# Two transformer blocks on one core: seven block products in the second feed forward, q and k projected together, and a later `out` in the latent attention

## The chip, the cores and the metric

The kernel runs on one core of a Trainium2 chip, as one program. The time is device microseconds of one execution; a kernel's time is the median of its runs. The engines are TensorE (PE), VectorE (DVE), ScalarE (ACT), GpSimd (POOL) and the queue of SyncE (SP), which issues most transfers. PSUM is the memory that matmuls write, SBUF the memory that all engines work from.

## The reference

The input is x, 512 tokens by 1024 features, in fp32. Two blocks follow each other.

```python
def first_block(x, ...):
    xn = rms_norm(h, norm_mix_pre)
    proj = xn @ w_in
    ...
    o_a = mixer_dilated(qkv_a, pos) @ w_o_a
    o_b = mixer_mla(q_c, kv_c, k_pe, pos, ...) @ w_o_b
    mix = (g_a * o_a + g_b * o_b) @ w_out
    h = h + rms_norm(mix, norm_mix_post)
    hn = rms_norm(h, norm_mlp_pre)
    ff = jnp.square(jax.nn.relu(hn @ w_ff1)) @ w_ff2
    h = h + rms_norm(ff, norm_mlp_post)

def second_block(x, ...):
    ...
    h = h + rms_norm_2(mix, ln_mix_post[l])
    a = rms_norm_2(h, ln_ffn_pre[l])
    ff = (jax.nn.silu(a @ w_ffn_gate[l]) * (a @ w_ffn_up[l])) @ w_ffn_down[l]
    h = h + rms_norm_2(ff, ln_ffn_post[l])
```

Block 1 mixes by a dilated attention (12 heads of 64 in three groups; q and k are rotated in their first 16 features) and by a latent attention (8 heads, 512 keys), and has a feed forward with a hidden width of 4096. Block 2 mixes by four recurrent or attention mixers and has a gated feed forward with a hidden width of 2816, which is 22 tiles of 128.

## The kernel before

The program has four phases: block 1's mixers (`mix1`, `mixers1`), its feed forward (`ffn1`), block 2's mixers (`mix2`) and its feed forward (`ffn2`).

**A matmul in three passes.** Each fp32 operand is kept as a high part and a low part. `mm3` (L318) forms a product as three matmuls into one PSUM tile: high by high (L320), high by low (L321) and low by high (L322). `wload` (L282) brings a weight unit of up to 128x1024 on SP's queue into `wraw` (3 buffers); ACT casts it to `whi` (L300) and DVE subtracts to get `wlo` (L301), five buffers each (`WB`). PSUM has four accumulators `acc` and two tiles each of `mps` and `ops`.

**Feed forward of block 2.** `groups` (L1193) walks over groups of hidden tiles, FF2 = (8, 6, 4, 4). For each tile a gate unit and an up unit of 24 matmuls of 512 columns run; `sink` in `ffn2` (L2194) multiplies by the token scale (DVE L2207), takes silu (ACT L2208), multiplies by the up product (DVE L2214) and splits into `hidh`, `hidl` (ACT L2215, DVE L2216). The units of the next group's first tile (two units) are run ahead, and then the group's down products come: for each column half f and each of four token blocks j one accumulator, whose content `Post.part` moves to `y` in SBUF: ACT copies in group 0 (L595), DVE adds in later groups (L597). The last group's products go through `sink`, `done` and the output transfers of `Post`.

**Block 1's projections.** `proj_qk` (L842) makes q or k of a head group in four chunks, one per 128 tokens: 24 matmuls of 256 columns, ACT's scaling of the result (L852), a rotation of four instructions on POOL (L688 to L691), and, as `turn`, transposes on PE (L860) whose results ACT and DVE copy out. `Fill` (L450) hands the chunks out one at a time between the items of the dilated attention; a chunk's `turn` comes after the next chunk. The numbers in `fills` say how many chunks stand before which item, and PE's order there is the order of the code.

**Latent attention.** Its 32 items (`ItemB`) are a head and a block of 128 queries each. `scores` is one matmul (L1092), then the maximum on DVE (L1095), the exponential on ACT (L1099) and the division on DVE (L1101). `turn`, two steps later, transposes P (PE L1106) into an `mps` tile and copies it to PT (L1107), by DVE for even items and by ACT for odd ones. `out`, one step later, multiplies by v (PE L1122); it does two items at once, on the odd one's step.

```python
            lag = 1 if n < 16 else 2
            while turned < len(items) and turned <= n - lag:
                items[turned].turn()
                turned += 1
            while outed < turned and outed <= n - lag - 1:
                items[outed].out()
                outed += 1
```

## Time and profile before

| | |
|---|---|
| median of 3 runs | 1525.47 us (1524.91 to 1526.32) |
| the profiled execution | 1524.67 us, its span 1522.9 us |
| PE busy | 1478.0 us (97%) |
| DVE busy | 788.6 us (52%) |
| ACT busy | 583.7 us (38%) |
| POOL busy | 246.2 us (16%) |

The span is what the profiler recorded of the execution, from the first instruction to the last. Busy times of engines overlap each other. A PE that is busy all the time still loses time with every matmul it need not do; the duration of one matmul in the trace overlaps its neighbours, so that what one costs is read from the distance of starts.

### The profile page before, as it was taken

The page shows a single profiled execution, that of the slowest core. Times are in us where ns is not written, and L with a number is a line of the kernel's source. Part 1 is how long each engine was busy: PE and PEld are TensorE (multiplying, and loading weights), DVE is VectorE, ACT ScalarE, POOL GpSimd, SP SyncE. Part 2 cuts the span into 40 slices and gives each one's busy share as a digit, 9 for nine tenths or more (in the row PEclk, how much of TensorE's full clock was granted, in tenths as well). Part 3 has the DMA queues.
Part 4 walks back from the last instruction along what each step waited for, and adds up shares of the span by engine and source line. Part 5 has one row for each costly group of instructions (what it writes and reads, how often), then busy time and mean ns, then how long its engine had stood idle before and what let it go on. Part 6 is the DMA issues. An engine that isn't in the chain of part 4 may idle for free.

```text
span 1522.9 us, 21857 instructions
## 1 busy us (share of the span) xinstructions
PE 1478.0 (97%) x8516; PEld 1240.6 (81%) x8520; DVE 788.6 (52%) x1569; ACT 583.7 (38%) x1099; POOL 246.2 (16%) x514
## 2 busy tenths in 40 slices
PE   8999999999999999999998999889999999999997
PEld 7999976678888888888887999667788888888885
DVE  6433367743746533434446686857656441434446
ACT  7344454533325442423225343533535323222222
POOL 0321210000201377203700052411000000000000
PEclk9999999999999999999999999979999999999999
DMA  8332121022225332322324423001124322423232
GB/s 302 132 100 75 45 64 42 33 80 97 90 91 179 119 97 70 119 85 87 110 93 141 146 88 116 32 29 42 42 90 161 124 97 59 136 83 111 83 97 84
DMA packets 54728, 147.37 MB, mean 97 GB/s; under 512 B 9824, under 2 KB 16368, under 8 KB 54624
## 3 DMA queue, kind: packets, MB, share of 16 engines
q1 hardware_dynamic: 52384, 143.38, 28.8%
q10 hardware_dynamic: 1776, 1.85, 0.4%
q8 instruction: 67, 1.10, 0.3%
q0 software_dynamic: 464, 0.74, 0.2%
q14 instruction: 37, 0.30, 0.1%
HBM read 135.12 MB, written 11.06 MB: 96 GB/s over the span
## 4 chain that ended last, share of the span: by engine, by line
PE 87%; DVE 9%; ACT 3%; issue 1%; DMA 1%; SPq 0%; DVEq 0%; ACTq 0%
PE acc L320 25%; PE acc L321 24%; PE acc L322 24%; DVE wlo L301 1%; PE acc L1092 1%; PE ops L1032 1%; PE ops L1122 1%; DVE y L625 1%; PE ops L320 1%; PE ops L322 1%; PE ops L321 1%; ACT whi L300 1%; PE acc L1977 1%; PE ops L1993 1%; PE acc L978 1%
## 5 line engine op out<-in xcount | busy, mean ns | idle before, releaser
L300 ACT CAST whi<-wraw 128x1024 fp32r<-128x1024 f32 (+4 forms) x237 | 234.5, 993 | 486.3 <-PE acc L321 226.6
L301 DVE TENSOR_TENSOR wlo<-wraw,whi 128x1024 fp32r<-128x1024 f32 (+4 forms) x237 | 282.2, 1195 | 233.7 <-ACT whi L300 224.1
L320 PE MATMUL acc<-xh,whi 128*128 128x512 f32 (+1 forms) x920 | 348.4, 380 | 7.2 <-ACT whi L300 5.3
L322 PE MATMUL acc<-xh,wlo 128*128 128x512 f32 (+1 forms) x920 | 343.5, 374 | 1.5 <-DVE wlo L301 1.5
L321 PE MATMUL acc<-xl,whi 128*128 128x512 f32 (+1 forms) x920 | 344.6, 375 | 0.3 <-DVE xl L664 0.3
L320 PEld LDWEIGHTS acc<-xh,whi 128*128 128x128 f32 x920 | 174.4, 190 | 44.1 <-ACT whi L300 7.5
L322 PEld LDWEIGHTS acc<-xh,wlo 128*128 128x128 f32 x920 | 174.2, 189 | 33.3 <-DVE wlo L301 2.1
L321 PEld LDWEIGHTS acc<-xl,whi 128*128 128x128 f32 x920 | 174.6, 190 | 31.7 <-issue 1.0
L320 PE MATMUL acc<-whi,hidh 128*128 128x512 f32 x432 | 169.0, 394 | 0.0
L321 PE MATMUL acc<-wlo,hidh 128*128 128x512 f32 x432 | 168.7, 393 | 0.0
L322 PE MATMUL acc<-whi,hidl 128*128 128x512 f32 x432 | 168.4, 392 | 0.0
L320 PE MATMUL acc<-whi,xh 128*128 128x256 f32 (+2 forms) x448 | 131.3, 293 | 0.2 <-ACT mv L1779 0.2
L321 PE MATMUL acc<-wlo,xh 128*128 128x256 f32 (+2 forms) x448 | 127.9, 285 | 0.0
L322 PE MATMUL acc<-whi,xl 128*128 128x256 f32 (+2 forms) x448 | 127.7, 285 | 0.0
L321 PEld LDWEIGHTS acc<-wlo,hidh 128*128 128x128 f32 x432 | 81.2, 188 | 18.3
L322 PEld LDWEIGHTS acc<-whi,hidl 128*128 128x128 f32 x432 | 81.2, 188 | 18.1
L320 PEld LDWEIGHTS acc<-whi,hidh 128*128 128x128 f32 x432 | 81.2, 188 | 17.9
L320 PEld LDWEIGHTS acc<-whi,xh 128*128 128x128 f32 x448 | 86.1, 192 | 2.8 <-issue 1.1
L321 PEld LDWEIGHTS acc<-wlo,xh 128*128 128x128 f32 x448 | 86.2, 192 | 0.1
L322 PEld LDWEIGHTS acc<-whi,xl 128*128 128x128 f32 x448 | 86.0, 192 | 0.0
L1252 POOL TENSOR_TENSOR relu<-relu 128x512 f32<-128x512 f32 (+1 forms) x37 | 36.9, 1005 | 230.6 <-ACT hidh L1251 226.5
L597 DVE TENSOR_TENSOR y<-acc,y 128x512 f32<-128x512 f32 x48 | 33.1, 689 | 63.1 <-PE acc L322 62.9
(535 smaller groups left out, 2151.9 us busy)
## 6 DMA issues: line engine op xcount, KB each, us to landing
wraw<-in_wp_dram SPq DMA_DIRECT2D x211, 512.0 KB, 3.5
hd<-y SPq DMA_DIRECT2D x24, 256.0 KB, 3.9
hr<-hd SPq DMA_DIRECT2D x12, 512.0 KB, 5.1
hr<-in_xt_dram SPq DMA_DIRECT2D x8, 512.0 KB, 5.5
H<-in_xT_dram SPq DMA_DIRECT2D x8, 256.0 KB, 4.6
wraw<-in_wp_dram SPq DMA_DIRECT2D x16, 128.0 KB, 3.7
gain<-in_gv_dram SPq DMA_DIRECT2D x8, 256.0 KB, 4.1
out_dram<-y SPq DMA_DIRECT2D x8, 256.0 KB, 2.1
```

Of the source, the lines that this page charges most:

```text
L300: ACT.copy(hi[:, s], raw[:, s])
L301: eng.tensor_tensor(lo[:, s], raw[:, s], hi.bitcast(F32)[:, s], op=OP.subtract)
L320: PE.matmul(ps, lhsT=w[0], rhs=x[0], start=first, stop=False)
L321: PE.matmul(ps, lhsT=w[0], rhs=x[1], start=False, stop=False)
L322: PE.matmul(ps, lhsT=w[1], rhs=x[0], start=False, stop=last)
L597: DVE.tensor_tensor(y, ps, y, op=OP.add)
L625: DVE.scalar_tensor_tensor(y, y, self.r[:, i:i + 1], self.hs[i][:, 512 * f:512 * f + 512], op0=OP.mult, op1=OP.add)
L978: PE.matmul(Sv[:, jj, a], lhsT=QKV[g]["q"][a][rr, 128 * j:128 * j + 128], rhs=QKV[g]["k"][a][rr, k0:k0 + W], start=False, stop=(jj == step ...
L1032: PE.matmul(po[:, j % 2, h], lhsT=PTv[0:w, jj, a, b], rhs=QKV[g]["v"][v][0:w, 64 * h:64 * h + 64], start=(b == 0), stop=(b == self.nb - 1))
L1092: PE.matmul(S, lhsT=qT[2 * p + e][0:96, 128 * i:128 * i + 128], rhs=kT[2 * (p % 2) + e][0:96], start=True, stop=True)
L1122: PE.matmul(po[64 * f:64 * f + 64, 128 * i:128 * i + 128], lhsT=VB[kt][:, 64 * h:64 * h + 64], rhs=PT[:, 128 * kt:128 * kt + 128], start=F ...
L1252: POOL.tensor_tensor(a, a, a, op=OP.mult)
```

## The change

Three things are changed.

**Seven products.** FF2 becomes (4, 4, 4, 4, 2, 4). In the first four groups the down product of 512 tokens by 512 hidden features (four tiles) by 1024 columns is cut in halves in each direction, and the eight block products are replaced by seven products of sums of blocks. `Pairs` forms the sums of the activations on POOL, per pair of hidden tiles, and splits them (ACT casts, DVE low parts). `seven` loads four weight quarters into tiles `wq` and forms the sums of them on POOL, in place. Each product has two token blocks of two hidden tiles in three passes. `Post.seven` keeps the seven products in SBUF (copied in group 0, added to in groups 1 to 3), and `Post.joined`, once after group 3, forms the eight outputs from them by 14 sums on POOL.

**q and k.** `proj_qk(g)` projects q and k of a head group at once: four chunks of 24 matmuls of 512 columns rather than eight of 256. Four weight units take the place of two and two. A chunk is turned by four transposes into one `mps` tile, copied out in four pieces. `fills` is adapted so that the same has been projected before each item.

**Order of the latent attention.** `out` of an item comes one step later, and the call of `weights_a` that depends on the count of items done comes with it.

```diff
-FF2 = (8, 6, 4, 4)
+FF2 = (4, 4, 4, 4, 2, 4)
+SEVEN = {"down": range(4)}
...
+        cols = lambda nm: list(range(qkv[nm] + 256 * g, qkv[nm] + 256 * g + 256))
+        for h in range(4):
+            u[f"Aqk{g}", h] = ("w_in", rows(2 * h, 2), cols("q") + cols("k"))
+        c = cols("v")
+        if g == 0:
+            c += list(range(3072, 3104))
+        for h, (k0, n) in enumerate(TMK[len(c)]):
+            u[f"Av{g}", h] = ("w_in", rows(k0, n), c)
...
+        def seven(self, g, i, j, ps):
+            if g == 0 and j == 0:
+                if i in (2, 6):
+                    t = gpool.tile([128, D], F32, name="hr", tag="hr", bufs=2)
+                    ts = [t[:, 0:512], t[:, 512:1024]]
+                elif i == 7:
+                    ts = [u("p7", tag="g") for _ in range(2)]
+                else:
+                    r, f = {1: (0, 0), 3: (0, 1), 4: (2, 0), 5: (2, 1)}[i]
+                    ts = [self.ys[r + t][f] for t in range(2)]
+                self.p[i] = ts
+            s = self.p[i][j]
+            if g == 0:
+                ACT.copy(s, ps)
+            else:
+                DVE.tensor_tensor(s, ps, s, op=OP.add)
+        def joined(self):
+            for j in range(2):
+                more = lambda a, b: POOL.tensor_tensor(self.p[a][j], self.p[a][j], self.p[b][j], op=OP.add)
+                more(6, 1)
+                more(1, 2)
+                more(3, 5)
+                more(7, 6)
+                more(3, 6)
+                more(4, 7)
+                more(5, 7)
...
-        def proj_qk(g, nm):
-            us = wrows(f"A{nm}{g}", 256)
-            res = QKV[g][nm] = [u(f"{nm}T", tag="g"), u(f"{nm}T", tag="g")]
-            tps = {}
+        def proj_qk(g):
+            us = ktiles([wload([(f"Aqk{g}", h)])[0] for h in range(4)], 0, 512)
+            for nm in ("q", "k"):
+                QKV[g][nm] = [u(f"{nm}T", tag="g"), u(f"{nm}T", tag="g")]
+            res = QKV[g]["q"] + QKV[g]["k"]
             for j in range(4):
                 ps = acc()
-                lin_tm(ps[:, 0:256], xs, tokpick(j), us, 0, 256)
-                if j % 2 == 0:
-                    tt = u("tm")
-                t = tt[:, 256 * (j % 2):256 * (j % 2) + 256]
-                ACT.activation(t, ps[:, 0:256], AF.Copy, scale=r_tm[:, j:j + 1])
-                rope(t.rearrange("p (h d) -> p h d", h=4)[:, :, 0:16], rp("ropeA", j, 32), 16, POOL)
+                lin_tm(ps, xs, tokpick(j), us, 0, 512)
+                t = u("tm")
+                ACT.activation(t, ps, AF.Copy, scale=r_tm[:, j:j + 1])
+                rope(t.rearrange("p (h d) -> p h d", h=8)[:, :, 0:16], rp("ropeA", j, 32), 16, POOL)
 
                 def turn(j=j, t=t):
-                    if j % 2 == 0:
-                        tps[j] = mps().rearrange("p (a x) -> p a x", a=2)
-                    tpv = tps[j - j % 2]
-                    for a in range(2):
-                        PE.transpose(tpv[:, a, 128 * (j % 2):128 * (j % 2) + 128], t[:, 128 * a:128 * a + 128], ident)
-                    if j % 2:
-                        for a in range(2):
-                            dst, src = res[a][:, 128 * (j - 1):128 * (j + 1)], tpv[:, a]
-                            if g:
-                                dst = res[a].rearrange("p (r x) -> p r x", r=4)[:, :, 32 * (j - 1):32 * (j + 1)]
-                                src = src.rearrange("p (x r) -> p r x", r=4)
-                            (ACT.copy if a == 0 else DVE.tensor_copy)(dst, src)
+                    tp = mps().rearrange("p (a x) -> p a x", a=4)
+                    for a in range(4):
+                        PE.transpose(tp[:, a], t[:, 128 * a:128 * a + 128], ident)
+                    for a in range(4):
+                        dst, src = res[a][:, 128 * j:128 * j + 128], tp[:, a]
+                        if g:
+                            dst = res[a].rearrange("p (r x) -> p r x", r=4)[:, :, 32 * j:32 * j + 32]
+                            src = src.rearrange("p (x r) -> p r x", r=4)
+                        (DVE.tensor_copy if a % 2 else ACT.copy)(dst, src)
                 yield turn
...
-            fill.plan.extend([proj_v(g), proj_qk(g, "q"), proj_qk(g, "k")])
+            fill.plan.extend([proj_v(g), proj_qk(g)])
         fill.plan.extend([mixed([proj_qr(), proj_vb()], (0, 0, 1, 0, 1, 0, 1, 1)), proj_pair(0)] + [gate(m, "g") for m in order[0:2]])
-        fill(14)
+        fill(10)
         rows_b()
         shared_k()
         items = [ItemA(0, j, e) for j in range(4) for e in range(2)]
         items += [ItemA(g, j, e) for g in (1, 2) for j in (0, 2) for e in range(2)]
         items += [ItemB(p, i, e) for p in range(4) for i in range(4) for e in range(2)]
-        fills = [2, 1, 2, 1, 2, 1, 2, 1] + [3] * 4 + [4, 4, 3, 2]
+        fills = [1] * 8 + [2] * 4 + [4, 4, 3, 2]
         fills += [0] * 32
         turned = outed = 0
-        for n in range(len(items) + 4):
+        for n in range(len(items) + 5):
...
-            while outed < turned and outed <= n - lag - 1:
+            while outed < turned and outed <= n - lag - (1 if n < 16 else 2):
...
+        def pair(self, p, a, b):
+            t0, t1 = HALF
+            x, y = u("sx"), u("sy")
+            POOL.tensor_tensor(x[:, t0], a[:, t1], b[:, t1], op=OP.add)
+            POOL.tensor_tensor(x[:, t1], x[:, t0], a[:, t0], op=OP.subtract)
+            POOL.tensor_tensor(y[:, t0], a[:, t0], a[:, t1], op=OP.subtract)
+            POOL.tensor_tensor(y[:, t1], b[:, t0], x[:, t1], op=OP.subtract)
+            if p[1] == 0:
+                self.first[p[0]] = u("a0h", F32R, tag="g"), u("a0l", F32R, tag="g")
+            a0 = tuple(t[:, HALF[p[1]]] for t in self.first[p[0]])
+            ACT.copy(a0[0], a[:, t0])
+            DVE.tensor_tensor(a0[1], a[:, t0], a0[0].bitcast(F32), op=OP.subtract)
+            bs, xs, ys = (split(t, tag="g", nm="pr") for t in (b, x, y))
+            half = lambda s, t: tuple(v[:, t] for v in s)
+            self.ops[p] = {1: a0, 2: half(bs, t0), 4: half(bs, t1), 5: half(xs, t0), 6: half(xs, t1),
+                           7: half(ys, t0), 3: half(ys, t1)}
+            self.mark = self.mark or last(mybir.EngineType.Activation)
...
+    def seven(nm, g, pairs, post):
+        W = {}
+        for r, f in ((0, 0), (1, 0), (1, 1), (0, 1)):
+            W[r, f] = CTX.up.tile([128, 1024], F32, name="wq", tag="wq", bufs=4)
+            o = UOFF[(nm, g), r, f]
+            with tc.issue_after(pairs.mark):
+                nc.sync.dma_start(out=W[r, f], in_=A["wp"][o:o + 128 * 1024].rearrange("(p n) -> p n", p=128))
+        A0, B0, B1, t = W[0, 0], W[1, 0], W[1, 1], W[0, 1]
+        def parts(raw):
+            hi, lo = (wpool.tile([128, 1024], F32R, name=n, tag=n, bufs=WB[1]) for n in ("whi", "wlo"))
+            ACT.copy(hi, raw)
+            DVE.tensor_tensor(lo, raw, hi.bitcast(F32), op=OP.subtract)
+            return [(hi[:, 512 * i:512 * i + 512], lo[:, 512 * i:512 * i + 512]) for i in range(2)]
+        def weights():
+            yield 1, parts(A0)
+            yield 2, parts(B0)
+            POOL.tensor_tensor(t, B1, t, op=OP.subtract)
+            yield 7, parts(t)
+            POOL.tensor_tensor(t, t, A0, op=OP.add)
+            yield 6, parts(t)
+            POOL.tensor_tensor(B0, B0, t, op=OP.subtract)
+            POOL.tensor_tensor(t, B1, t, op=OP.subtract)
+            yield 4, parts(B0)
+            yield 5, parts(t)
+            yield 3, parts(B1)
+        for i, w in weights():
+            for j in range(2):
+                ps = ops() if i == 7 else acc()
+                for k in range(2):
+                    xh, xl = pairs.ops[g, k][i]
+                    c = slice(128 * j, 128 * j + 128)
+                    mm3(ps, (xh[:, c], xl[:, c]), w[k], k == 0, k == 1)
+                post.seven(g, i, j, ps)
...
+                seven(nm, g, pairs, post)
+                if g + 1 not in SEVEN[nm]:
+                    post.joined()
+                n0 += n
+                continue
...
+            a = sil[m][:, ts]
+            DVE.tensor_tensor(a, a, ps, op=OP.mult)
+            if pairs.add(m, sil[m], ts):
+                return
...
-    with phase("m1", u=10, z=12):
+    with phase("m1", u=11, z=12):
...
-    with phase("f2", u=6):
+    with phase("f2", u=8):
```

How the instructions stand is shown at three places. On PE, in the latent attention (scores L1092, turn L1106, out L1122; L1127, L1141 and L1157 after the change), before the change:

```order
L1106 MATMUL mps_2893<-cstt_72,P_2805 128x128 x4
L1092 MATMUL acc_2900<-kT_526,qT_2562 128x512
L1106 MATMUL mps_2909<-cstt_72,P_2846 128x128 x4
L1117 LDWEIGHTS identb_73
L1117 MATMUL ops_2916<-zero_539,identb_73 128x512
L1122 MATMUL ops_2916<-PT_2851,vb_518 64x128
L1122 MATMUL ops_2916<-PT_2894,vb_518 64x128
```

`out` reads PT_2894, which comes from the turn into mps_2893, with one scores matmul and one turn between the two. After the change, where the turn into mps_2533 is that of PT_2534 (the rows left out are the rest of the earlier `out`):

```order
L1141 MATMUL mps_2533<-cstt_72,P_2449 128x128 x4
L1157 MATMUL ops_2343<-PT_2438,vb_518 64x128
...
L1127 MATMUL acc_2552<-kT_526,qT_2214 128x512
L1141 MATMUL mps_2561<-cstt_72,P_2498 128x128 x4
L1127 MATMUL acc_2568<-kT_527,qT_2217 128x512
L1141 MATMUL mps_2577<-cstt_72,P_2514 128x128 x4
L1152 LDWEIGHTS identb_73
L1152 MATMUL ops_2584<-zero_539,identb_73 128x512
L1157 MATMUL ops_2584<-PT_2503,vb_518 64x128
L1157 MATMUL ops_2584<-PT_2534,vb_518 64x128
```

There two turns and two scores stand between a turn and the `out` that reads it.

On DVE, during a group's down products in block 2's feed forward (L597 evicts an accumulator, L301 makes a low part of weights), before the change:

```order
L597 TENSOR_TENSOR y_10850<-acc_12875,y_10850 128x512
L597 TENSOR_TENSOR y_10852<-acc_12889,y_10852 128x512
L597 TENSOR_TENSOR y_10854<-acc_12903,y_10854 128x512
L301 TENSOR_TENSOR wlo_13036<-wraw_13034,whi_13035 128x1024
L597 TENSOR_TENSOR y_10856<-acc_12917,y_10856 128x512
L301 TENSOR_TENSOR wlo_13072<-wraw_13070,whi_13071 128x1024
L597 TENSOR_TENSOR y_10851<-acc_12943,y_10851 128x512
L597 TENSOR_TENSOR y_10853<-acc_12957,y_10853 128x512
L597 TENSOR_TENSOR y_10855<-acc_12971,y_10855 128x512
L301 TENSOR_TENSOR wlo_13106<-wraw_13104,whi_13105 128x1024
L597 TENSOR_TENSOR y_10857<-acc_12985,y_10857 128x512
```

and after it, in the fourth group, where L624 evicts a product and L1285 and L309 make the low parts of a weight sum and of a loaded weight:

```order
L624 TENSOR_TENSOR y_10504<-acc_12503,y_10504 128x512
L1285 TENSOR_TENSOR wlo_12596<-wq_12489,whi_12595 128x1024
L624 TENSOR_TENSOR hr_11140<-acc_12515,hr_11140 128x512
L624 TENSOR_TENSOR hr_11140<-acc_12523,hr_11140 128x512
L624 TENSOR_TENSOR p7_11162<-ops_12536,p7_11162 128x512
L1285 TENSOR_TENSOR wlo_12616<-wq_12487,whi_12615 128x1024
L624 TENSOR_TENSOR p7_11163<-ops_12544,p7_11163 128x512
L309 TENSOR_TENSOR wlo_12652<-wraw_12650,whi_12651 128x1024
L624 TENSOR_TENSOR hr_11185<-acc_12557,hr_11185 128x512
L624 TENSOR_TENSOR hr_11185<-acc_12565,hr_11185 128x512
L309 TENSOR_TENSOR wlo_12686<-wraw_12684,whi_12685 128x1024
```

Where eight evictions stood among low parts there are fourteen, about two to each low part.

On POOL, which had nothing in this phase, the first group's rows after the change (L1291, L1293, L1295 and L1296 are the sums of weights, L1255 to L1258 those of activations):

```order
L1291 TENSOR_TENSOR wq_11107<-wq_11105,wq_11107 128x1024
L1255 TENSOR_TENSOR sx_10891<-sil_10677,sil_10681 128x256
L1257 TENSOR_TENSOR sy_10892<-sil_10677 128x256
L1256 TENSOR_TENSOR sx_10891<-sx_10891,sil_10677 128x256
L1258 TENSOR_TENSOR sy_10892<-sil_10681,sx_10891 128x256
L1255 TENSOR_TENSOR sx_11013<-sil_10738,sil_10978 128x256
L1257 TENSOR_TENSOR sy_11014<-sil_10738 128x256
L1256 TENSOR_TENSOR sx_11013<-sx_11013,sil_10738 128x256
L1293 TENSOR_TENSOR wq_11107<-wq_11107,wq_11101 128x1024
L1258 TENSOR_TENSOR sy_11014<-sil_10978,sx_11013 128x256
L1295 TENSOR_TENSOR wq_11103<-wq_11103,wq_11107 128x1024
L1296 TENSOR_TENSOR wq_11107<-wq_11105,wq_11107 128x1024
```

The last sum of the second pair of tiles (L1258) stands behind the second sum of weights (L1293).

## Rows read from the trace of the kernel before

**Rows 1.** the page: span; section 1, busy time by engine

```profile
span 1522.9 us, 21857 instructions
PE 1478.0 (97%) x8516; PEld 1240.6 (81%) x8520; DVE 788.6 (52%) x1569; ACT 583.7 (38%) x1099; POOL 246.2 (16%) x514
```

**Rows 2.** busy time by stage: length, then each engine, granted clock, DMA share

```profile
216.00:325.00 109.00, 104.19 (x652) 73.12 (x656) 77.95 (x177) 52.69 (x106) 5.35 (x5) 1.00 0.15 49
1160.00:1506.00 346.00, 346.00 (x1607) 289.70 (x1606) 140.68 (x190) 100.50 (x135) 0.00 (x0) 1.00 0.29 94
```

**Rows 3.** PE's timeline in block 2's feed forward: start, duration; 12 apart

```profile
1300.05 0.39 PE L320 MATMUL acc<-xh,whi 128*128 128x512 f32 x1
...
1302.77 0.39 PE L320 MATMUL acc<-xh,whi 128*128 128x512 f32 x1
```

**Rows 4.** PE's timeline in block 1's q projection; 22 apart

```profile
58.35 0.28 PE L321 MATMUL acc<-wlo,xh 128*128 128x256 f32 x1
...
60.98 0.28 PE L322 MATMUL acc<-whi,xl 128*128 128x256 f32 x1
```

**Rows 5.** costs by shape, block 2's feed forward (1170 to 1500 us)

```profile
L301 DVE TENSOR_TENSOR wlo<-wraw,whi 128x1024 fp32r<-128x1024 f32 x61 | 74.5, 1225 | 49.2 <-ACT whi L300 45.7
L597 DVE TENSOR_TENSOR y<-acc,y 128x512 f32<-128x512 f32 x16 | 11.0, 690 | 24.4 <-PE acc L322 24.4
L300 ACT CAST whi<-wraw 128x1024 fp32r<-128x1024 f32 x61 | 64.1, 1054 | 198.5 <-PE acc L321 80.5 <-issue 69.6 <-PE acc L322 46.0
L2215 ACT CAST hidh<-sil 128x512 fp32r<-128x512 f32 x20 | 12.4, 622 | 4.8 <-DVE sil L2214 4.8
```

**Rows 6.** costs by shape on POOL, block 1's feed forward (476 to 822 us)

```profile
L1252 POOL TENSOR_TENSOR relu<-relu 128x512 f32<-128x512 f32 x27 | 28.8, 1067 | 155.7 <-ACT hidh L1251 151.6 <-DVE wlo L301 4.1
L1252 POOL TENSOR_TENSOR relu<-relu 128x256 f32<-128x256 f32 x8 | 6.1, 780 | 21.2 <-ACT hidh L1251 21.2
```

**Rows 7.** timeline of POOL and of DVE side by side, same stretch

```profile
593.06 0.29 POOL L1274 TENSOR_TENSOR s5t<-s5s,s5b 128x64 f32<-128x64 f32 x1
593.42 1.19 POOL L1275 TENSOR_TENSOR s5t<-s5t 128x64 f32<-128x64 f32 x1
593.12 1.30 DVE L301 TENSOR_TENSOR wlo<-wraw,whi 128x1024 fp32r<-128x1024 f32 x1 [0.18 <-ACT whi L300]
...
617.84 1.04 POOL L1252 TENSOR_TENSOR relu<-relu 128x512 f32<-128x512 f32 x1 [4.06 <-DVE wlo L301]
```

**Rows 8.** DVE's adds from PSUM, block 1's feed forward (480 to 800 us)

```profile
L597 DVE TENSOR_TENSOR y<-acc,y 128x512 f32<-128x512 f32 x32 | 22.0, 688 | 38.7 <-PE acc L322 38.5
```

**Rows 9.** the page: DMA issues, KB each, us to landing

```profile
wraw<-in_wp_dram SPq DMA_DIRECT2D x211, 512.0 KB, 3.5
```

**Rows 10.** costs by shape, projections of block 1 (42 to 140 us)

```profile
L852 ACT ACTIVATE tm<-acc,r_tm 128x256 f32<-128x256 f32 x16 | 7.6, 477 | 22.8 <-PE acc L322 22.8
L691 POOL TENSOR_TENSOR tm<-rope 128x64 f32<-128x64 f32 x16 | 8.1, 506 | 1.2
```

**Rows 11.** PE's groups in the latent attention (216 to 325 us)

```profile
L1122 PE MATMUL ops<-PT,vb 128*64 128x128 f32 x256 | 21.7, 281 | 3.6 <-ACT PT L1107 3.0
L1106 PE MATMUL mps<-cstt,P 128*128 128x128 f32 x128 | 19.3, 274 | 1.1 <-DVE P L1101 1.1
```

**Rows 12.** PE's timeline around one of its waits there

```profile
259.88 0.63 PE L1106 MATMUL mps<-cstt,P 128*128 128x128 f32 x4 [0.35 <-DVE P L1101]
260.44 0.43 PE L1122 MATMUL ops<-PT,vb 128*64 128x128 f32 x2
261.56 1.09 PE L1122 MATMUL ops<-PT,vb 128*64 128x128 f32 x14 [0.69 <-ACT PT L1107]
```

**Rows 13.** ACT and DVE around the same wait

```profile
260.92 0.59 ACT L1107 COPY PT<-mps 128x512 f32<-128x512 f32 x1
261.12 0.49 DVE L1101 TENSOR_SCALAR P<-P,rl 128x512 f32<-128x512 f32 x1
...
263.74 0.69 DVE L1095 TENSOR_REDUCE mxb<-acc 128x1 f32<-128x512 f32 x1 [0.74 <-PE acc L1092]
```

More of the change, by code (lines that the diff above doesn't have):

```diff
@@ L42, in _units @@
     for g in range(3):
-        for nm in ("q", "k", "v"):
-            c = list(range(qkv[nm] + 256 * g, qkv[nm] + 256 * g + 256))
-            if nm == "v" and g == 0:
-                c += list(range(3072, 3104))
-            for h, (k0, n) in enumerate(TMK[len(c)]):
-                u[f"A{nm}{g}", h] = ("w_in", rows(k0, n), c)
+        cols = lambda nm: list(range(qkv[nm] + 256 * g, qkv[nm] + 256 * g + 256))
[6 more added lines that the diff above has]
+            u[f"Av{g}", h] = ("w_in", rows(k0, n), c)
     for m in range(6):
@@ L72, in grouped @@
             k0 = sum(sizes[:g])
-            if g + 1 < len(sizes):
+            if g in SEVEN.get(nm, ()):
+                for r in range(2):
+                    for f in range(2):
+                        u[(nm, g), r, f] = (w, [128 * (k0 + r + 2 * i) for i in range(2)],
+                                            list(range(512 * f, 512 * f + 512)))
+            elif g + 1 < len(sizes):
                 output((nm, g), w, range(k0, k0 + n))
@@ L578, in __init__ @@
             self.hs = {}
+            self.p = {}
         def scaled(self, pre):
@@ L1191, in mixers1, with __init__, add @@
         return gates, OA, OB
-    def groups(sizes, tiles, xs, sink, carry, nm, hid, post, nxt, between=()):
+    class Pairs:
+        def __init__(self, nm, sizes):
+            self.a, self.n, self.first, self.ops, m = {}, {}, {}, {}, 0
+            self.mark = None
+            self.of = {}
+            for g, n in enumerate(sizes):
+                if g in SEVEN[nm]:
+                    self.of.update({m + i: (g, i // 2) for i in range(n)})
+                m += n
+        def add(self, m, a, ts):
+            if m not in self.of:
+                return False
+            p = self.of[m]
+            self.a.setdefault(p, {})[m] = a
+            self.n[p] = self.n.get(p, 0) + ts.stop - ts.start
+            if self.n[p] == 2 * T:
+                a = self.a.pop(p)
+                self.pair(p, *(a[m] for m in sorted(a)))
+            return True
+        def pair(self, p, a, b):
[15 more added lines that the diff above has]
+            self.mark = self.mark or last(mybir.EngineType.Activation)
@@ L1196, in groups @@
+    def groups(sizes, tiles, xs, sink, carry, nm, hid, post, nxt, between=(), pairs=None):
         n0 = 0
@@ L1208, in groups @@
                     between[g]()
+            if g in SEVEN.get(nm, ()):
+                seven(nm, g, pairs, post)
[3 more added lines that the diff above has]
+                continue
             hs = [hid[m] for m in ms]
@@ L2212, in sink @@
             hi, lo = (t[:, ts] for t in hid[m])
-            a = sil[m][:, ts]
-            DVE.tensor_tensor(a, a, ps, op=OP.mult)
             ACT.copy(hi, a)
             DVE.tensor_tensor(lo, a, hi.bitcast(F32), op=OP.subtract)
-        po = Post("ln_ffn_post_2", old, new, "u")
+        po, pairs = Post("ln_ffn_post_2", old, new, "u"), Pairs("down", FF2)
         groups(FF2, lambda m: [("gate", m), ("up", m)], pre.xs, sink, carry, "down", hid, po, None,
-               [lambda: po.scaled(pre.r)])
+               [lambda: po.scaled(pre.r)], pairs)
     hd = [dram.tile([T, D], F32, name=f"hd{i}") for i in range(3)]
-    with phase("m1", u=10, z=12):
+    with phase("m1", u=11, z=12):
         carry = mix1(hd[0])
```

## The prediction

> **What bounds the kernel now.** I read the page first: TensorE (PE) is busy 1478.0 of the 1522.9 us [rows 1], so time goes only where PE gets less work or waits less. Then the busy time by stage [rows 2]: in block 2's feed forward PE is busy 346.00 of 346.00 us at full clock, while VectorE (DVE) works 140.68, ScalarE (ACT) 100.50 and GpSimd (POOL) 0.00; in block 1's latent attention PE is busy 104.19 of 109.00 and DVE 77.95. The first stage pays only for matmuls taken away, the second also for a wait taken away. PE's timeline tells what a matmul costs; the durations in the costs by shape are overlapped and too long for that. From 1300.05 to 1302.77 us twelve matmuls of 512 columns start [rows 3]: 2.72 / 12 = 0.2267 us each. In block 1's projection 22 steps of 256 columns take 60.98 - 58.35 = 2.63 us [rows 4]: 0.1195 each, more than half of 0.2267.
>
> **Part 1, seven products in block 2's down projection.** A group of four hidden tiles now takes 7 products x 2 token blocks x 2 tiles x 3 passes = 84 matmuls of 512 columns; as `part` does it, it takes 8 outputs x 4 x 3 = 96. Four groups save 48 matmuls, and the count of gate and up matmuls stays: 48 x 0.2267 = **10.9 us off PE**, all of it on the path while PE stays without gaps. Added on the side, per group:
> - POOL: four sums of 128x1024 weights, eight half-tile sums of 128x256. A sum of 128x1024 is not in the trace. 128x64 takes 0.29 us and 128x512 takes 1.04 [rows 7], so a straight line gives an estimate of 1.9 us; the contended mean of 1.067 for 128x512 [rows 6] doubled gives 2.1. I take 1.9. The 128x256 sums take at most 0.78 [rows 6]. Sum 7.6 + 6.2 = 13.8 us of a group's 62.6 (eight gate and up units of 24 x 0.2267 = 5.44, and 19.0 for the 84).
> - ACT and DVE: seven casts and seven low parts where four stood, 1.05 and 1.23 us each [rows 5], and 14 evictions of 0.69 [rows 5] where eight stood. ACT's further casts of the operands are some 0.62 each [rows 5].
>
> The place to watch is the 19.0 us of the burst itself. DVE has 14 x 0.69 = 9.7 us of evictions there and, one weight buffer coming free with each product, seven low parts, 8.6: 18.3 of 19.0 us. It fits, and what keeps PE running is the run ahead. Let U be the end of a group's last up unit. Two units of the next group follow (10.9 us), so the burst starts at U + 10.9. Five weight buffers hold those two units, A0 and B0 at U; the freed fifth takes the third weight: cast and low part end by U + 2.3, POOL's next sum by U + 4.2, the cast of it waits for a buffer until U + 5.4, its low part ends by U + 7.7 and POOL's last sum by U + 9.6, ahead of the burst. The fifth weight is cast at U + 10.9, ready at U + 13.2 and wanted four products of 2.72 later, at U + 21.8: 8.6 us in hand, the same for those behind it. An eviction waits at most behind one low part and its cast, 2.3 us, while four accumulators of 1.36 us each stand between. The operand sums of the last pair (POOL 0.78 each, cast 0.62, low part 0.69) follow the POOL sum that ends at U + 4.2, so they end by about U + 8 and are wanted for the third product at U + 16.3. I cost all this at nothing. Without the run ahead a derived weight costs 1.9 + 1.05 + 1.23 = 4.2 us less the 2.7 of one product, 1.5 us each. For the part I keep a bound of 4 x 3 = 12 us of loss.
>
> The loads: four of 512 KB per group as before, 3.5 us each [rows 9], on SP's queue. The fourth of a group waits until B1 of the group before has been read, some U + 18.6, and behind it queue weights for a unit that starts four units after the burst, U + 29.9 + 21.8 = U + 51.7. Nothing. The 14 joining sums on POOL (14 x 1.07 = 15 us [rows 6], up to 23 if DVE's two-operand work of about 8 us in that stretch holds them off) have four units, 21.8 us, before the next `part` adds to the same tiles: nothing, at worst 1 us, once.
>
> **Part 2, q and k together.** 576 matmuls of 256 columns become 288 of 512: 576 x 0.1195 - 288 x 0.2267 = 68.8 - 65.3 = **3.5 us off PE**. The 48 transposes stay 48. Per chunk ACT scales once instead of twice (0.48 each [rows 10]) and POOL's rotation runs four times instead of eight, with up to 0.51 us each at half the width [rows 10]; both have the next chunk, 5.4 us, before the transposes want them. POOL then does less in sum, so nothing. Three weight buffers changing to four per group could make a first chunk wait for its last weights; a cast and a low part are 2.3 us against 5.4 of a chunk: nothing, at worst 2 us at each of five boundaries.
>
> **Part 3, the latent attention's `out` one step later.** PE waits there 3.6 us ahead of L1122 and 1.1 ahead of L1106 [rows 11]. One wait in full: after two of the sixteen matmuls PE stops from 260.44 to 261.56 [rows 12], since ACT begins the copy of PT at 260.92 and ends at 261.51 [rows 13]. The turn that now precedes `out` is bound by almost the same moment: its P is scaled by DVE from 261.12 to 261.61 [rows 13], and its PSUM buffer is the one that ACT copies out. What PE can do meanwhile is the next scores, about 0.5 us of the 1.1. But DVE, which idles 0.74 us at 263.74 for those scores [rows 13], gets them earlier. So of the 3.6 us I take **2.0**; the ends are 0 (DVE is the bound) and 3.6. The 1.1 stays. `weights_a`, a step later, still has five steps before `combine_a`: nothing.
>
> **Sum.** 10.9 + 3.5 + 2.0 = 16.4 us. The profiled execution took 1524.67 us, so 1508.3; the median of the runs is 0.8 higher, 1525.47: **1509 us**.
>
> **Rivals.**
> - *The bursts are short of DVE* (0.13). For it: 18.3 of 19.0 us. Against: 8.6 us in hand. One to three us per burst give back 4 to 12: 1513 to 1521 us.
> - *Only the matmuls pay* (0.08). DVE's 77.95 of 109 us [rows 2] swallows part 3, and buffer waits in part 2 take some of its gain: 10.9 + 3.5 - 5 to 10.9 + 3.5 - 0, so 1511 to 1516.
> - *POOL and DVE shut each other out, and it is slower* (0.07). A POOL sum of 128x64 that took 0.29 us at 593.06 took 1.19 at 593.42, beside DVE's low part from 593.12 to 594.42 [rows 7], and ended 0.19 after it. If POOL's four weight sums ran in the burst and held off the low parts in turn, DVE's 18.3 us would become 18.3 + 7.6 = 25.9, 6.9 over the burst; four times 27.5 us: 1509 + 27.5 = 1536. It decides against the change once a burst loses 16.4 / 4 = 4.1 us. Against it: the working above ends POOL's sums at U + 9.6, before the burst, and DVE's adds from PSUM, over half its load there, took 0.688 us beside a working POOL [rows 8] and 0.690 beside an idle one [rows 5].
> - *It does not save what it says* (0.04): PE's gaps are not the columns', and 1522 to 1527 follow.
>
> [...]
>
> **How the numbers follow.** Forecast 0.68, between 1504 and 1513: part 3 at 0 to 3.6, small waits up to 3. A measurement of this kernel can tell about 0.2%, 3 us, from no change. The range 1503 to 1517 holds the forecast, the second rival and half of the first, some 0.83. Faster: the forecast, the second rival and all but a little of the first, 0.88; same: the last rival and that little, 0.05; slower: the third, 0.07.
>
> **What would show it.** Right: PE busy without gaps in the bursts, block 2's feed forward 10.9 us shorter; the projections 3.5 us shorter with 0.2267 us between matmuls; idle ahead of `out`'s matmuls gone and that ahead of the turn's not above 2.7. Wrong: PE idle ahead of the seven products, released by DVE's low parts or by POOL's sums; DVE's low part above 1.4 us in the mean; idle of PE at the start of each q and k chunk.

## The result and the profile after

The changed kernel took 1512.74 us (median of four runs, 1506.46 to 1514.12) against 1525.31 before: a ratio of 0.990 (0.987 to 0.993). Measured twice more beside the experiments, it took 1506.01 us against 1525.45 (0.987, 0.986 to 0.989) and 1508.87 against 1526.49 (0.989, 0.987 to 0.991). So it is faster, by 12.6 to 19.4 us or about 1%; 1509 was forecast, 1503 to 1517 the range. The profile shown here is of a run of 1511.7 us. The page's span and section 1, beside [rows 1]:

```profile
span 1510.0 us, 21333 instructions
PE 1464.1 (97%) x8180; PEld 1217.4 (81%) x8184; DVE 866.2 (57%) x1641; ACT 605.6 (40%) x1131; POOL 333.0 (22%) x528
```

Busy time by stage (length, each engine, granted clock, DMA share): the latent attention, which answers to the first of [rows 2], the head of block 2's feed forward, and the rest of it, which answers to the second.

```profile
215.20:311.10 95.90, 92.57 (x620) 65.42 (x623) 75.19 (x174) 51.34 (x104) 5.76 (x5) 1.00 0.15 48
1155.00:1175.00 20.00, 17.95 (x137) 17.75 (x137) 10.66 (x23) 7.83 (x15) 2.22 (x1) 0.91 0.16 53
1175.00:1490.00 315.00, 315.00 (x1405) 261.38 (x1404) 203.85 (x209) 115.10 (x151) 97.38 (x61) 1.00 0.29 93
```

In the last of these stretches PE is busy in every microsecond, and from start to start no matmul of 512 columns there takes over 0.236 us (0.2267 in the mean), although POOL now works 97 us and DVE 0.65 of the time where it was 0.41. The loss sits in the 20 us ahead of it: 2 us of idle, at a granted clock of 0.91, which is the mean of 0.50 from 1159.4 to 1162.8 us and 1.00 before and behind that.

To see where the time went, I cut each run at starts of the same matmuls: the first transpose of block 1's projections, the first scores of the latent attention, its last `out`, the first transpose of block 2, the head of block 2's feed forward (L658 before, L697 after) and the last matmul of all. For the last stage the cuts are these rows of PE's timeline, first before:

```profile
1139.89 0.49 PE L658 MATMUL mps<-cstt,y 128*128 128x128 f32 x3
...
1511.99 0.39 PE L322 MATMUL acc<-whi,hidl 128*128 128x512 f32 x1
```

and after:

```profile
1134.14 0.38 PE L697 MATMUL mps<-cstt,y 128*128 128x128 f32 x2
...
1499.01 0.39 PE L330 MATMUL acc<-whi,hidl 128*128 128x512 f32 x1
```

So that stage went from 372.10 us to 364.87. The stages in us, one profiled execution of each kernel (the rest of block 1 with its feed forward, between the fourth and the fifth column, takes 506.4, in out_only 507.1; the labels are those of the experiments):

| kernel | up to the first transpose | projections, block 1 | latent attention | block 2's mixers | block 2's feed forward |
|---|---|---|---|---|---|
| before | 51.85 | 164.68 | 102.12 | 314.83 | 372.10 |
| after | 52.94 | 162.26 | 95.74 | 316.80 | 364.87 |
| after_again | 53.02 | 162.17 | 96.11 | 312.40 | 363.35 |
| after_five | 53.84 | 162.25 | 95.65 | 314.09 | 363.06 |
| seven_only | 53.73 | 164.69 | 102.25 | 315.19 | 362.67 |
| qk_only | 59.66 | 162.27 | 102.03 | 312.72 | 372.70 |
| out_only | 53.41 | 164.68 | 95.75 | 314.86 | 372.10 |
| no_lead | 53.73 | 162.32 | 95.95 | 312.51 | 366.52 |
| later_five | 52.69 | 162.27 | 95.64 | 313.06 | 361.23 |
| later_act_five | 53.06 | 160.68 | 96.32 | 314.54 | 361.22 |

For the same code (after, after_again, after_five) the projections and the latent attention repeat to within 0.5 us. The first column and the mixers do not, and they don't follow the change. Of the 5.6 us between the profiled executions of after and after_again, which are of the measurements of 1512.74 and 1506.01 us, 4.4 lie in the mixers (the last section has the clock) and 1.5 in the feed forward. The forecast by stage was -3.5, -2.0, 0, -10.9; the changed kernel shows -2.4, -6.0 to -6.5, +2.0 to -2.4, -7.2 to -9.0.

**The head of block 2's feed forward.** PE's timeline shows the new wait, between a matmul into `ops` and the next transposes, which wait for ACT's R, itself made from the norm's `rsq`:

```profile
1156.12 0.28 PE L330 MATMUL ops<-xh,wlo 128*128 128x256 f32 x1
...
1158.45 0.66 PE L697 MATMUL mps<-cstt,y 128*128 128x128 f32 x4 [2.05 <-ACT R L717]
```

Side by side, what POOL and DVE did (L561 is a step of the reciprocal root in the norm ahead of the feed forward, on a 128x1 column):

```profile
1154.86 2.36 POOL L1291 TENSOR_TENSOR wq<-wq 128x1024 f32<-128x1024 f32 x1 [101.01 <-DVE xl L703]
```

```profile
1154.31 0.17 DVE L551 TENSOR_SCALAR rsq<-rsq 128x2 f32<-128x2 f32 x1
...
1154.78 2.46 DVE L561 SCALAR_TENSOR_TENSOR rsq<-rsq 128x1 f32<-128x1 f32 x2
1157.16 0.47 DVE L703 SCALAR_TENSOR_TENSOR xl<-mps,pv,xh 128x256 fp32r<-128x256 f32 x1
...
1157.73 0.35 DVE L561 SCALAR_TENSOR_TENSOR rsq<-rsq 128x1 f32<-128x1 f32 x2
```

The same two instructions take 2.46 us beside POOL's first sum of weights and 0.35 us a moment later. The sum needs nothing but two loads, so it runs as soon as these have landed, in the middle of the norm on which everything behind waits. The last of the four loads lands at 1154.694 us here and the sum begins at 1154.858, 0.16 us later; in the three groups that follow, the same sum begins 0.16 us behind its last load as well. (The releaser that the sum's row names is DVE's; in seven_only, below, the row names the load.)

**The bursts.** DVE's and POOL's costs by shape, block 2's feed forward (1175 to 1490 us):

```profile
L309 DVE TENSOR_TENSOR wlo<-wraw,whi 128x1024 fp32r<-128x1024 f32 x43 | 58.8, 1368 | 8.7 <-ACT whi L308 7.8
L1285 DVE TENSOR_TENSOR wlo<-wq,whi 128x1024 fp32r<-128x1024 f32 x28 | 50.6, 1807 | 4.4 <-PE ops L330 2.4 <-ACT whi L1284 1.9
L624 DVE TENSOR_TENSOR y<-acc,y 128x512 f32<-128x512 f32 x24 | 15.4, 677 | 0.0
```

```profile
L1296 POOL TENSOR_TENSOR wq<-wq 128x1024 f32<-128x1024 f32 x4 | 10.9, 2718 | 4.9 <-DVE wlo L1285 4.9
L1293 POOL TENSOR_TENSOR wq<-wq 128x1024 f32<-128x1024 f32 x4 | 9.6, 2393 | 0.0
```

Low parts of weights that took 1.225 us before [rows 5] take 1.37 and 1.81 in the mean, evictions from PSUM 0.677 against 0.690, and a sum of 128x1024 2.4 to 2.8 (L1291's), not 1.9. Nobody on PE's path notices, by the steps between starts above.

**The latent attention.** PE's groups there, as in [rows 11]:

```profile
L1141 PE MATMUL mps<-cstt,P 128*128 128x128 f32 x128 | 19.2, 273 | 2.7 <-DVE mxb L1131 2.4 <-DVE P L1136 0.3
L1157 PE MATMUL ops<-PT,vb 128*64 128x128 f32 x256 | 17.3, 279 | 0.6
```

The idle time ahead of `out` falls from 3.6 to 0.6 us and that ahead of the turn grows from 1.1 to 2.7, a net of 1.4; the stage is shorter by 6.4. Most of the rest is in the busy column: 21.7 to 17.3 us for the same 256 matmuls.

Of the new wait ahead of the turn the profile puts 2.4 us, three waits, down to DVE's scaled maximum (L1131). The transposes don't read that; they read P, and in all three DVE's division of P (L1136) has ended some 0.14 us before PE goes on. One of them, DVE's rows and then PE's:

```profile
254.37 0.48 DVE L1136 TENSOR_SCALAR P<-P,rl 128x512 f32<-128x512 f32 x1
254.76 0.21 DVE L1131 TENSOR_SCALAR mxb<-mxb,rq 128x1 f32<-128x1 f32 x1
```

```profile
254.99 0.63 PE L1141 MATMUL mps<-cstt,P 128*128 128x128 f32 x4 [0.80 <-DVE mxb L1131]
```

**The projections.** PE's timeline has one wait that was not there, and DVE's shows what it was busy with (L902 copies the transposes out, L727 to L730 rotate the queries of the latent attention):

```profile
177.89 0.60 PE L896 MATMUL mps<-cstt,tm 128*128 128x128 f32 x4
179.92 0.63 PE L1049 MATMUL mps<-cstt,P 128*128 128x128 f32 x4 [1.43 <-DVE rope L729]
```

```profile
177.93 0.22 DVE L729 TENSOR_TENSOR rope<-tm,ropes 128x64 f32<-128x64 f32 x1
...
178.54 0.29 DVE L902 COPY qT<-mps 128x128 f32<-128x128 f32 x1
178.74 0.49 DVE L730 TENSOR_TENSOR tm<-rope 128x128 f32<-128x128 f32 x2
...
179.48 0.28 DVE L902 COPY kT<-mps 128x128 f32<-128x128 f32 x1
```

L729, which PE's row names, had ended at 178.15 us; the last of the copies, which frees the PSUM tile, ends at 179.76, and PE goes on at 179.92.

### The profile page after: what moved, and what is told of

Same layout as the page of the kernel before. It is cut to its first block, busy times and chain, and to the rows that moved or that the text cites. A ratio compares the mean times of both kernels' runs of the same rounds, so it can differ in the third digit from the quotient of the medians.

```text
span 1510.0 us, 21333 instructions
## 1 busy us (share of the span) xinstructions
PE 1464.1 (97%) x8180; PEld 1217.4 (81%) x8184; DVE 866.2 (57%) x1641; ACT 605.6 (40%) x1131; POOL 333.0 (22%) x528
## 5 line engine op out<-in xcount | busy, mean ns | idle before, releaser
L309 DVE TENSOR_TENSOR wlo<-wraw,whi 128x1024 fp32r<-128x1024 f32 (+4 forms) x221 | 269.4, 1225 | 160.4 <-ACT whi L308 152.3
L328 PE MATMUL acc<-whi,hidh 128*128 128x512 f32 x304 | 119.6, 395 | 0.0
L329 PE MATMUL acc<-wlo,hidh 128*128 128x512 f32 x304 | 119.2, 394 | 0.0
L330 PE MATMUL acc<-whi,hidl 128*128 128x512 f32 x304 | 118.9, 394 | 0.0
L328 PE MATMUL acc<-whi,xh 128*128 128x256 f32 (+3 forms) x352 | 114.5, 325 | 0.2 <-ACT mv L1902 0.2
L329 PE MATMUL acc<-wlo,xh 128*128 128x256 f32 (+3 forms) x352 | 111.7, 317 | 0.0
L330 PE MATMUL acc<-whi,xl 128*128 128x256 f32 (+3 forms) x352 | 111.6, 317 | 0.0
L329 PEld LDWEIGHTS acc<-wlo,hidh 128*128 128x128 f32 x304 | 57.2, 188 | 13.2
L330 PEld LDWEIGHTS acc<-whi,hidl 128*128 128x128 f32 x304 | 57.2, 188 | 13.2
L328 PEld LDWEIGHTS acc<-whi,hidh 128*128 128x128 f32 x304 | 57.2, 188 | 13.0
L1284 ACT CAST whi<-wq 128x1024 fp32r<-128x1024 f32 x28 | 29.5, 1055 | 62.1 <-PE acc L329 44.9
```

What stands on the lines that cost most here:

```text
L309: eng.tensor_tensor(lo[:, s], raw[:, s], hi.bitcast(F32)[:, s], op=OP.subtract)
L328: PE.matmul(ps, lhsT=w[0], rhs=x[0], start=first, stop=False)
L329: PE.matmul(ps, lhsT=w[0], rhs=x[1], start=False, stop=False)
L330: PE.matmul(ps, lhsT=w[1], rhs=x[0], start=False, stop=last)
L1284: ACT.copy(hi, raw)
```

## The experiments

**The three parts, one at a time.** seven_only is the changed kernel with the other two parts taken back; qk_only and out_only are the kernel before with one part each. The core of each, in that order:

```diff
-            fill.plan.extend([proj_v(g), proj_qk(g)])
+            fill.plan.extend([proj_v(g), proj_qk(g, "q"), proj_qk(g, "k")])
...
-            while outed < turned and outed <= n - lag - (1 if n < 16 else 2):
+            while outed < turned and outed <= n - lag - 1:
```

```diff
-            fill.plan.extend([proj_v(g), proj_qk(g, "q"), proj_qk(g, "k")])
+            fill.plan.extend([proj_v(g), proj_qk(g)])
```

```diff
-            while outed < turned and outed <= n - lag - 1:
+            while outed < turned and outed <= n - lag - (1 if n < 16 else 2):
```

> Only the seven products of block 2's down projection; block 1 is that of the kernel before. Prediction's theory: 48 matmuls of 0.2267 us gone and nothing given back, 10.9 us faster, about 1514.5. Theory from the trace after (POOL's first weight sum shuts DVE out for 2.4 us in the norm at the head of block 2's feed forward, and PE then runs a stretch at the lower clock): 10.9 minus about 3.6, so 7.3 faster, about 1518, with a small DVE operation of over 2 us beside the sum. Either can lie 2 to 5 us off by the clock in block 2's mixers.

> Only q and k of block 1 projected together. Prediction's theory: 3.5 us faster, about 1522. Theory from the trace after: 3.8 us off the matmuls, 1.4 given back where the softmax's transposes wait for a PSUM tile whose four copies out go by ACT and DVE in turn, so 2.4 faster, about 1523.

> Only the latent attention's out one step later. Prediction's theory: 2.0 us faster, at most 3.6, about 1523.5. Theory from the distances of starts in the trace after: the latent attention 6.4 us shorter, about 1519, since the short gaps within out's matmuls were waits too, which the page does not count as idle.

Measured: 1518.61, 1523.93 and 1521.25 us, ratios 0.995 (0.993 to 0.996), 0.998 (0.997 to 0.999) and 0.998 (0.996 to 1.000) to the kernel before. The stages say more than these, since the first column moves by up to 8 us in a profiled run (qk_only's). Each part acts in its own stage and adds up with the others: out_only's latent attention is 95.75 us, the changed kernel's 95.74; qk_only's projections 162.27 against 162.26. One stage moves beside its part: qk_only's feed forward is 0.6 us longer than before, by a wait of PE of 0.75 us in its head with POOL idle, where DVE's instructions stand in another order.

seven_only's feed forward is 362.67. There the sum of POOL begins at 1161.21 us and fell upon another instruction of the norm, a sum of two 128x2 tiles that took 1.61 us where it takes 0.16 in the changed kernel. POOL's row and DVE's:

```profile
1161.21 2.38 POOL L1293 TENSOR_TENSOR wq<-wq 128x1024 f32<-128x1024 f32 x1 [99.21 <-DMA wq<-in_wp_dram]
```

```profile
1161.38 0.48 DVE L701 SCALAR_TENSOR_TENSOR xl<-mps,pv,xh 128x256 fp32r<-128x256 f32 x1 [0.73 <-ACT xh L700]
1161.99 1.61 DVE L675 TENSOR_TENSOR msum<-mspre 128x2 f32<-128x2 f32 x1
```

The first of DVE's two, which takes one input from PSUM, runs its usual 0.48 us beside the sum; the second, with both inputs in SBUF, is held to the sum's end at 1163.59.

**The first sum of weights later.** If that sum causes the wait, it must go when the sum waits for the first pair's sums of activations, which come after the norm:

```diff
+            self.pmark = self.pmark or last(mybir.EngineType.Pool)
...
-            POOL.tensor_tensor(t, B1, t, op=OP.subtract)
+            with tc.issue_after(pairs.pmark):
+                POOL.tensor_tensor(t, B1, t, op=OP.subtract)
```

> The changed kernel with POOL's first weight sum of the first group queued behind the first pair's sums of activations; the loads stay where they are. If the sum shuts DVE out at the head of block 2's feed forward: the 2.3 us wait of PE there is gone and its stretch at the lower clock too, 3.6 us faster than the changed kernel, about 1509. If the four early loads of weights are what delays the head: no change.

Measured: 1506.55 us, 0.986 (0.984 to 0.989). Measured again, beside the changed kernel on the same chip:

> The changed kernel once more, beside the next two: by the profiles its second feed forward is 2.2 us longer than with the later sum (3.6 where the lower clock comes in as well), so about 2 us above the next.

> The first weight sum later, in five rounds: about 2 us below the changed kernel beside it, up to 3.6. If the clock in block 2's mixers decides alone: no difference between the two that their intervals show.

Measured: 1508.87 (0.989, 0.987 to 0.991) and 1505.78 us (0.986, 0.984 to 0.988), 3.1 apart. The intervals just overlap, but every run of the one (1503.95 to 1506.82) lies below every run of the other (1506.96 to 1516.45). In later_five's profile the new wait of PE in the head is gone; those of 0.76, 0.64 and 0.94 us that are left stand in the kernel before too. DVE's row beside a silent POOL is:

```profile
1150.69 0.34 DVE L561 SCALAR_TENSOR_TENSOR rsq<-rsq 128x1 f32<-128x1 f32 x2
```

The stage takes 361.20 to 361.23 us in the four runs with the later sum, 10.87 to 10.90 less than the 372.10 before; 48 x 0.2267 = 10.88 was predicted. Everything else that the seven products add is indeed hidden.

**Twice the sum, and a fill in its place.** double_sum computes the first group's first sum once more into a tile of its own, ahead of it; memset_sum leaves that sum out and puts two fills of the same tile in its place:

```diff
+            if g == 0:
+                e = CTX.up.tile([128, 1024], F32, name="ex", tag="ex", bufs=1)
+                POOL.tensor_tensor(e, B1, t, op=OP.subtract)
             POOL.tensor_tensor(t, B1, t, op=OP.subtract)
```

```diff
-            POOL.tensor_tensor(t, B1, t, op=OP.subtract)
+            if g == 0:
+                POOL.memset(t, 1.0)
+                POOL.memset(t, 2.0)
+            else:
+                POOL.tensor_tensor(t, B1, t, op=OP.subtract)
```

> The changed kernel with POOL's first weight sum of the first group done twice (the first time into a spare tile). If each sum shuts DVE out for its length: a second small DVE operation of over 2 us beside it, or one of some 4.7, and PE's wait at the head of block 2's feed forward grows from 2.3 us by about 2.4. If the sum only happens to lie there: PE's wait stays 2.3.

> The changed kernel with POOL's first weight sum of the first group left out and two fills of the same tile in its place, which POOL writes without reading SBUF (the first group's seventh product is left out in its meaning, not in its work). [...] If any busy POOL slows DVE, or if the early loads do it: PE waits some 2 us as before.

Measured: 1509.93 and 1508.09 us, one run each, feed forward 363.79 and 362.21 us. double_sum, POOL and then DVE:

```profile
1154.51 2.38 POOL L1293 TENSOR_TENSOR ex<-wq 128x1024 f32<-128x1024 f32 x1 [101.33 <-DVE rsq L561]
1156.97 2.35 POOL L1294 TENSOR_TENSOR wq<-wq 128x1024 f32<-128x1024 f32 x1
```

```profile
1154.76 2.15 DVE L565 SCALAR_TENSOR_TENSOR rsq<-rsq 128x2 f32<-128x2 f32 x1
1156.94 2.52 DVE L561 SCALAR_TENSOR_TENSOR rsq<-rsq 128x1 f32<-128x1 f32 x2
```

Each sum holds DVE to its own end: 1154.51 + 2.38 = 1156.89, and the held row ends at 1156.91. That was expected. That PE would wait for both was not borne out: its wait is 2.4 us (2.1 in after_again), and the stage is only 0.4 longer than there. While the first sum held DVE, PE still had matmuls to run; it waits from 1157.74 to 1160.11 us, beside the second. memset_sum's first fill runs from 1152.78 to 1153.74, its second from 1153.80 to 1154.76, and DVE beside them:

```profile
1153.10 0.66 DVE L545 TENSOR_SCALAR rsq<-msum 128x2 f32<-128x2 f32 x1
1153.80 0.98 DVE L550 TENSOR_SCALAR rsq<-rsq 128x2 int32<-128x2 int32 x1
```

These take 0.17 us in the changed kernel. A fill has no input (its row is `MEMSET wq<-`), and that it would hold nobody was a guess of mine; each of these two is held to the end of a fill, and PE waits 0.9 us, where some 2 were named for a POOL that slows DVE whatever it does. Both have one input. L677, with two, took its usual 0.16 us from 1152.90, beside the first fill. In after_again the sum itself held the second of them, L550, for 2.29 us.

**The transposes copied out by ACT alone.** With the sum later, all four copies of a chunk go to ACT, which is not behind the rotations:

```diff
-                        (DVE.tensor_copy if a % 2 else ACT.copy)(dst, src)
+                        ACT.copy(dst, src)
```

> The changed kernel with the first weight sum later, and q's and k's transposes copied out by ACT alone. If the copies by ACT and DVE in turn hold the PSUM tile at 178 us: the 1.4 us ahead of the softmax's transposes goes, 1.4 us faster than the later sum alone, about 1505. If DVE's rotation of the latent q holds PE there anyway: no change.

> The changed kernel once more, beside the others on one chip: about 3.6 us above the later sum. If what differs between its runs is the granted clock in block 2's mixers, its runs spread by some 7 us again, and a profile with a higher mean clock has a shorter stretch there.

> The later sum and the transposes of q and k copied out by ACT alone, in five rounds: 1.4 us below the later sum alone, so about 3.5 us below the changed kernel and about 21 us below the kernel before.

Measured: later_act 1505.43 us (0.987, 0.985 to 0.988) beside after_again's 1506.01; the second time 1504.46 (0.985, 0.983 to 0.987), the fastest version, 4.4 us below the changed kernel beside it and 22.0 below the kernel before. after_again missed its expectation: it is 0.6 us above later_act, not 5, and its four runs spread by 0.6 us, not 7. In the two profiles later_act has its gain in the projections (1.5) and in the feed forward (2.1) and loses 2.6 in the mixers and 0.9 ahead of the first transpose. The projections go from 162.2 to 160.68 us, and the wait is gone (PE's timeline of later_act):

```profile
178.91 0.60 PE L896 MATMUL mps<-cstt,tm 128*128 128x128 f32 x4
179.34 0.60 PE L1049 MATMUL mps<-cstt,P 128*128 128x128 f32 x4
```

The end-to-end gain of 1.3 us over later_five is less than the intervals resolve; the stage is what shows it.

**No run ahead.** The prediction held that the two units of the next group, which run ahead of a burst, keep PE fed. Here no unit runs ahead of the seven products:

```diff
-            lead = 1 if g + 1 < len(sizes) else 0
+            lead = 1 if g + 1 < len(sizes) and g not in SEVEN.get(nm, ()) else 0
```

> The changed kernel without the run ahead: in the four groups with seven products the next group's first tile comes after the products. If the run ahead of 10.9 us is what hides the sums, casts and low parts of weights and operands (with POOL and DVE shutting each other out): PE now waits ahead of the first product for the operands of the last tile and ahead of the third and later products for derived weights, 3 to 6 us in each of four groups, 12 to 24 us slower than the changed kernel. If a burst runs on its own pace: PE waits under 1 us per group.

Measured: 1510.1 us, one run; the feed forward is 366.52 us, 3.2 longer than after_again's, not 12 or more. PE's groups there (1168 to 1490 us) name some 1.3 us of idle, and by starts PE stands still five times for 0.3 to 0.8 us beyond the pitch of 0.2267, 2.1 in all:

```profile
L328 PE MATMUL acc<-xh,whi 128*128 128x512 f32 (+1 forms) x317 | 123.0, 388 | 1.0 <-DVE y L624 1.0
...
L328 PE MATMUL acc<-whi,prh 128*128 128x512 f32 x80 | 31.6, 395 | 0.3 <-DVE y L624 0.3
```

They wait for evictions, not for weights. The weights come about as early as with lead units: the first four of the second group's products are cast 21.7, 15.8, 10.8 and 5.4 us ahead of the burst, in the changed kernel 21.7, 16.3, 10.9 and 3.9. Eight more steps lie 0.07 to 0.11 us beyond the pitch, most of them straight behind one of the five, and add 0.75; so 2.9 of the 3.2 us are placed. A loss of 0.8 us per burst is what the expectation names for a burst that runs on its own pace.

## Why the prediction was right, and where it was not

- **Seven products: the 10.9 us is right**, to 0.02, once the sum is out of the head. The pitch of 0.2267 between starts, and not the 0.39 of a matmul's own row, was the right price.
- **"I cost all this at nothing" failed at one place.** The price of a sum was taken as 1.9 us, from a line through small shapes; it is 2.36 where it runs first. And I looked for POOL's contention with DVE in the bursts, where weights are wanted; it came in the norm ahead of them, and the stage lost 1.8 to 2.1 us by it (1.4 in seven_only), and 3.65 in the first profile, where the clock fell as well. The third rival had the mechanism and took the wrong place and some ten times the price (27.5 us): the low parts of the weight sums take 1.81 us and cost PE nothing, since the weights are cast well ahead of the burst (3.9 to 21.7 us in the second group). All low parts there take 1.54 in the mean, so one sign of being wrong, above 1.4, was met without the loss that it was to tell of.
- **POOL and DVE hold each other, in both directions.** DVE's 2.46 us beside POOL's 2.36 is one, and the trace of before showed the other (POOL's 1.19 us, [rows 7]). Which instructions of DVE are held is not shown: the two of 0.66 and 0.98 us beside the fills, and L550's 2.29 beside the sum, have one input, the 1.61 of L675 in seven_only has two, and L701 ran its 0.48 us there beside the same sum.
- **q and k: the matmuls gave 3.9, the stage 2.4.** From start to start the 576 matmuls take 70.64 us and the 288 take 66.70, where 68.8 and 65.3 were reckoned: the step behind the first matmul of a chunk is longer than the pitch (0.20 us where the others take 0.12, from 67.30 to 67.50 us before), and there are half as many chunks. So the term was 0.4 too small. What failed is "both have the next chunk ... so nothing": a new wait of 1.43 us takes part of the gain back. I counted ACT and POOL and forgot who copies the transposes out: DVE, whose queue has the rotations of another projection in front.
- **`out` a step later: 2.0 was mis-sized, 6.4 measured, above my upper end of 3.6.** The step that failed is the equation of a gain with a group's idle time. Its companion forecast, idle ahead of the turn not above 2.7, was just met (2.7), and the new wait is for DVE's division of P, as the prediction had it: the turn is bound by almost the same moment.
- **The run ahead is not what keeps PE running**: without it the stage loses 3.2 us, 0.8 per burst; the prediction's 1.5 for each derived weight, with 12 as bound, did not come, since the weights are cast ahead of the burst all the same.
- **Not in the sum**: block 2's mixers, 312.4 to 316.8 us for the same code.

So the time fell into the range with three terms off: 4.0 to 4.5 us more from `out`, 1.1 less from q and k, 1.9 to 3.7 less from the feed forward. The three stages together gave 16.0 to 17.9 us for the 16.4 of the sum; that they came so close is luck, since the errors of the terms go both ways.

## What to carry to other kernels

Work that is put on POOL to be out of the way can still hold DVE where the two meet (2.46 us for 0.35 here), so look not at the stage it is meant for but at when its inputs land: here an instruction that needs only loads ran 0.16 us after they had landed, in a serial norm; tied to something later, it left the stage its 10.9 us. Price a wait of PE by distances between starts, never by idle columns, when matmuls overlap: the latent attention got 6.4 us shorter where the columns gave 1.4. And when two steps are joined, list every instruction behind them and its queue, the copies out of PSUM too (1.43 us of wait here).

## What the runs showed of the hardware

- **PE's busy column hides waits.** The first `out` of 16 matmuls after 255.7 us, before and after, shows no idle in either row (PE's timelines, before first):

```profile
255.71 1.36 PE L1122 MATMUL ops<-PT,vb 128*64 128x128 f32 x16
257.00 0.70 PE L1092 MATMUL acc<-kT,qT 96*128 96x512 f32 x1
```

```profile
255.76 1.09 PE L1157 MATMUL ops<-PT,vb 128*64 128x128 f32 x16
256.79 0.70 PE L1127 MATMUL acc<-kT,qT 96*128 96x512 f32 x1
```

  To the next scores it is 1.29 us before and 1.03 after. After the change two heads' matmuls, each with 64 columns of weights, start 5 to 7 ns apart, and then 102 to 104 ns pass to the next two (in 15 of 113 cases 153 or 154); in the kernel before, many such pairs are pulled apart (the first of this group by 160 ns, from 255.71 to 255.87 us). From start to start within their groups all 256 take 20.28 us before and 13.20 after; out_only, where nothing but the order is changed, has the changed kernel's 17.3 us in the busy column.
- **The clock is not the code's alone.** Block 2's mixers have the same code in all three kernels; these are the windows from 895 to 1055 us of before, after and after_again (the granted clock is the third figure from the end):

```profile
895.00:1055.00 160.00, 147.81 (x1244) 119.23 (x1243) 118.36 (x224) 66.32 (x130) 46.96 (x52) 0.91 0.20 63
```

```profile
895.00:1055.00 160.00, 149.13 (x1231) 119.17 (x1230) 113.93 (x221) 65.65 (x128) 46.51 (x53) 0.89 0.19 59
```

```profile
895.00:1055.00 160.00, 149.21 (x1270) 121.05 (x1269) 115.82 (x230) 67.55 (x135) 46.51 (x53) 0.93 0.19 60
```

  0.89 goes with 316.8 us of mixers, 0.91 with 314.8, 0.93 with 312.4. Likewise a wait of some 2 us ahead of the feed forward was followed by 0.91 in the first profile and by 1.00 in after_again. What decides it between executions stays open.
- **A fill on POOL held DVE**, though it has no input (0.66 and 0.98 us for instructions of 0.17, in memset_sum, one run).
